# Where the last merge's raw weights lie, and when its sums begin, in a hybrid flow-matching step

## The chip, the cores and the metric

The kernel runs on one core of a Trainium2 chip. The metric is the device time in microseconds of one execution. Times inside the profiled execution count from the start of its span.

## The reference, cut to what matters

One layer with two branches (a long convolution and windowed attention) whose results are gated, projected, merged, projected once more and normalised. Only the end concerns us:

```python
def merge_branches(y_h, g_h, y_a, g_a, m, w_bh, w_ba, w_out):
    p_h = (y_h * jax.nn.silu(g_h)) @ w_bh
    p_a = (y_a * jax.nn.silu(g_a)) @ w_ba
    m_h, m_a = jnp.split(jax.nn.sigmoid(m), 2, axis=-1)
    return (m_h * p_h + m_a * p_a) @ w_out

def layer_forward(x, cond, ctx_kv, p):
...
    out = merge_branches(y_h, g_h, y_a.reshape(g_a.shape), g_a, m, p["w_bh"], p["w_ba"], p["w_out"])
    x_new = layer_norm(ALPHA * x + gate * out, p["ln_g"], p["ln_b"])
    return x_new, kv_out
```

There are 640 tokens (128 of context, 512 latent) and all widths are 1024.

## The kernel before

Activations lie transposed: channels in 128 partitions, 640 tokens along the free dimension, handled as two halves of 320. A matrix of 1024 x 1024 is eight weight tiles of 128 x 1024, numbered in one array `wall`: 80 to 87 are `w_bh` (`T_BH`), 88 to 95 are `w_ba` (`T_BA`), 96 to 103 are `w_out` (`T_WO`).

**Three matmuls for one.** For precision each fp32 operand is split into a high part, rounded to fp32r by a copy on ScalarE (ACT), and a low part, the difference from it, usually by a subtraction on VectorE (DVE). `split` (L100 to L102) does both. A product is then high·high + high·low + low·high. For some tiles the low part is made otherwise (L1163 to L1166): ACT writes the negated high part, and a transfer issued on GpSimd's queue (POOL) adds the raw weights to it from DRAM.

**Seven products for eight.** `pair_tile` (L1178) multiplies two neighbouring weight tiles `i0, i1` (four quarters a11, a12, a21, a22 of 128 x 512) with two halves of the tokens by a scheme of the Strassen-Winograd kind: seven products instead of eight, numbered j = 0 to 6 here, each of 12 matmuls of 320 columns (four K tiles, three parts each), so 84 for a pair. Four of the seven operands are sums of quarters, made on DVE by `wsum` in `prepare` (L1145) and put in tiles `s`; products 0, 4 and 5 use the quarters a11, a12, a22 as they are. `prep(j)` splits operand j into `wb[j]`. These tiles come from two rings, "wh" with two buffers (products 0, 3, 5) and "wl" with three (1, 2, 4, 6), so that product 5's place is free when product 0 of the same pair is done, and product 4's when product 6 of the pair before is done. `prep(j + 5)` for products 5 and 6 stands behind products 0 and 1; the rest stands in `prepare`. In this last merge, from the second pair on, operands 4 and 5 get their low part by the transfer on POOL.

The products are collected in four PSUM banks (`sp`, named x, y, v, z) by additions on DVE (L1204, L1210), and each finished quarter of the result goes to `use`. In the last merge that is `merged`: a gate on DVE in place of the row `ma` (L574), then `finish`, which adds the first branch's row `mh` (L1489) and splits the sum into the operands `mH, mL` of the output projection. The next pair's first product takes the bank that product 4 of this pair leaves, so it waits for that product's gate.

**The order.** TensorE's order inside the merge is that of the program. SP's loads are pinned in program order (`pinned`, L62 to L66), so a load that waits for its buffer holds back all loads behind it. The other engines' orders, and where output matmuls go among the merge's, are laid out ahead of time by a planner that simulates the program and takes, at each point, the first instruction in program order that would be ready. Each queue then runs strictly in that order. An instruction may be pinned behind what was traced before it on its engine; in `prepare` the first sum of the next pair (`wsum(2, ...)`) is.

**The stage.** First the eight tiles of `w_bh` (one `proj` each, 48 matmuls), with the rows of the attention branch loaded and split beside them, and in the end the first `w_ba` tiles loaded. `gate_bias` (L1433) adds a row to the output gates meanwhile; its raw row `b0` lies in the buffer with the tag "gr". Then four pairs of `w_ba`: (88, 89) is pair 0, (94, 95) pair 3. Raw tiles go through three buffers (tag "raw"). In the loop of `pair_tile`, each product yields twice, after its second K tile and at its end, so that the caller counts i = 0 to 13; `prepare` of the following pair stands behind product 3. The last pair starts loading and splitting the output weights (`out_weight`), whose raw tiles use the same three buffers and whose parts go where operands of the merge were. Then five output tiles of 128 tokens (`out_tile`) with a normalisation each.

Of the kernel before, what the change touches and what calls it, by code (L numbers as in the profile page):

```python
# [9 lines left out]
F32 = mybir.dt.float32  # L10
F32R = mybir.dt.float32r
# [4 lines left out]
D = 1024  # L16
# [3 lines left out]
NT = 640  # L20
# [25 lines left out]
def tile_hyena_natten_step(ctx: ExitStack, tc: tile.TileContext, a, o):  # L46
# [15 lines left out]
    def load_to(dst, src):  # L62
        ins = nc.sync.dma_start(dst, src)
        last[:] = [ins]
        if pinned[0]:
            tc.keep_in_program_order(ins)  # L66
# [33 lines left out]
    def split(dst_h, dst_l, src, eng=None):  # L100
        hi = nc.scalar.activation(dst_h, src, AF.Copy)  # L101
        return hi, (eng or nc.vector).tensor_tensor(dst_l, src, f(dst_h), op=ALU.subtract)  # L102
# [30 lines left out]
    def wraw(i):  # L133
        raws[i] = wp.tile([P, 1024], F32, tag="raw", bufs=3, name=f"raw{i}")
        load_to(raws[i][:], a["wall"][i])
# [1006 lines left out]
    def prepare(i0, i1, pin):  # L1142
        for i in (i0, i1):
            if i not in raws:
                wraw(i)  # L1145
                loads[i] = last[0]
        ra, rb = raws.pop(i0), raws.pop(i1)
        a11, a12, a21, a22 = (r[:, 512 * h : 512 * h + 512] for r in (ra, rb) for h in range(2))
        src = {0: a11, 4: a12, 5: a22}
        wb = {}  # L1150
        s_cols = 512 if i0 >= T_BH else NT

        def wsum(j, x, y, op, dst=None):
            src[j] = dst if dst is not None else sp.tile([P, s_cols], F32, tag="s", bufs=3 if i0 >= T_BH else 2, name=f"s{j}_{i0}")[:, :512]
            ins = nc.vector.tensor_tensor(src[j], x, y, op=op)  # L1155
            if pin and j == 2:
                tc.keep_in_program_order(ins)

        def prep(j):
            if j > 6:  # L1160
                return
            wb[j] = wp.tile([P, 2, 512], F32R, tag=RING[j % 5], bufs=2 if RING[j % 5] == "wh" else 3, name=f"wb{i0}_{j}")
            if i0 > T_BA and j in (4, 5):  # L1163
                nc.scalar.activation(wb[j][:, 1], src[j], AF.Copy, scale=-1.0)
                nc.gpsimd.dma_start(wb[j][:, 1], a["wall"][i0 + (j == 5)][:, 512 * (j > 0) : 512 * (j > 0) + 512], accum_op=ALU.add)
                high[i0, j] = nc.scalar.activation(wb[j][:, 0], src[j], AF.Copy)  # L1166
            else:
                high[i0, j] = split(wb[j][:, 0], wb[j][:, 1], src[j])[0]

        wsum(2, a11, a21, ALU.subtract)  # L1170
        wsum(1, src[2], a22, ALU.subtract)
        for j in range(3):
            prep(j)
        wsum(3, a21, a22, ALU.add)
        wsum(6, a12, src[1], ALU.add, src[1])
        for j in range(3, 5):
            prep(j)
        ready[i0] = wb, prep  # L1178

    def pair_tile(i0, i1, use, operand=operand):  # L1180
        def halfrow(tag, bufs, name):
            return sp.tile([P, HALF if i0 >= T_BH else 384], F32, tag=tag, bufs=bufs, name=f"{name}{i0}")[:, :HALF]

        if i0 not in ready:
            prepare(i0, i1, False)
        wb, prep = ready.pop(i0)
        ps = {}
        for j in range(7):
            if j < 4:
                ps["xyvz"[j]] = acc(f"sp{i0}_{j}")[:, :HALF]  # L1190
            dst, x = ps["xyvzxvz"[j]], operand(ORDER[j])
            for k in range(4):
                wh, wl = (wb[j][:, i, P * k : P * k + P] for i in range(2))
                for i, (wk, xi) in enumerate(((wh, 0), (wh, 1), (wl, 0))):
                    nc.tensor.matmul(  # L1195
                        dst, wk, x(xi, k), start=j < 4 and k == 0 and i == 0, stop=k == 3 and i == 2, skip_group_check=True,
                    )
                if k == 1:
                    yield
            if j == 0:  # L1200
                u = halfrow("u", 1, "u")
                nc.scalar.activation(u, dst, AF.Copy)
            elif j == 1:
                nc.vector.tensor_tensor(u, dst, u, op=ALU.add)  # L1204
            elif j == 4:
                use(0, 0, dst)
            else:
                if j != 3:
                    c = halfrow("c", 4, f"c{j}_")
                after = nc.vector.tensor_tensor(c, dst, c if j == 3 else u, op=ALU.add)  # L1210
                if j != 2:
                    use(*{3: (1, 1), 5: (1, 0), 6: (0, 1)}[j], c)
            prep(j + 5)
            if j == 3 and i0 in GATED_AT:
                gate_row(after)
                gate_load()
            if j == 3 and (i0, i1) in follow:
                prepare(*follow[i0, i1], True)
            yield

# [155 lines left out]
    nc.gpsimd.memset(eps[:], LN_EPS)  # L1376
    ts = {t: [lp.tile([P, 4, HALF], F32R, tag=f"{t}{i}", name=f"ya_{t}{i}") for i in range(2)] for t in ("t4", "t2", "t3", "t1")}

    def out_weight(k):
        raw = wp.tile([P, D], F32, tag="raw", bufs=3, name=f"wo{k}")  # L1380
        load_to(raw[:], a["wall"][T_WO + k])
        if k in (0, 1, 2, 4):
            t = {0: "t2", 1: "t3", 2: "t1", 4: "t4"}[k]
            wh, wl = (lp.tile([P, 4 * HALF], F32R, tag=f"{t}{i}", name=f"wo{k}_{i}")[:, :D] for i in range(2))
        elif k == 3:
            wh = slot(0, "v", f"woh{k}", F32R)[:, :D]
            wl = gp.tile([P, D], F32R, tag="gr", name=f"wol{k}")[:]
        else:
            if k == 5:
                wh = hp.tile([P, NK * NT], F32R, tag="hH", name="woh5")[:, :D]  # L1390
            else:
                wh = wp.tile([P, D], F32R, tag="wh", name=f"woh{k}")[:]
            if k == 5:
                wl = wp.tile([P, D], F32R, tag="raw", bufs=3, name="wol5")[:]
            else:
                wl = wp.tile([P, D], F32R, tag="wl", bufs=3, name=f"wol{k}")[:]
        wo[k] = wh, wl
        split(wh, wl, raw[:])

    def turned_sums(k):  # L1400
        b11, b12 = (ya_raw[k][:, cs] for cs in CS)
# [47 lines left out]
    with tc.manual_schedule(engines={mybir.EngineType.PE}):  # L1449
        for gen in firsts:  # L1450
            for _ in range(4):
                next(gen)
        firsts = [now(gen) for gen in firsts]
        for n in range(NK):
            ps = firsts[n] if n < 2 else now(proj(T_BH + n, yhH, yhL))
            wraw(T_BH + n + 2)
            if n % 2 == 0:
                mhp.append(mp.tile([P, 2 * NT], F32, tag=f"mh{n}", name=f"mh{n}"))
            load_to(mh(n), mh_d[n])
            for p, cs in zip(ps, CS):  # L1460
                gate(mh(n)[:, cs], p)
            if n < NK - 2:
                early[T_BH + n + 2] = wtile(T_BH + n + 2)
            ya_row(YA[n])
            if n == 0:
                gb = gate_bias()
            if n >= 2:
                next(gb, None)
        mH, mL = yhH, yhL

        mas, pending = {}, []

        def ma(n):
            if n // 2 % 2:
                mas[n] = slot(1, ("q", "ql")[n % 2], f"ma{n}")
            else:
                mas[n] = row(mp, "ma", f"ma{n}", bufs=2)
            load_to(mas[n][:], ma_d[n])

        def merged(n, hf, src):  # L1480
            th = mas[n][:, CS[hf]]
            gate(th, src)
            pending.append((n, hf, th))

        def finish():
            if not pending:
                return
            n, hf, th = pending.pop(0)
            nc.vector.tensor_tensor(th, th, mh(n)[:, CS[hf]], op=ALU.add)  # L1489
            split(mH[n][:, CS[hf]], mL[n][:, CS[hf]], th)  # L1490

        first_out = {3: 0, 5: 1, 7: 2, 9: 3}
        pairs = [(T_BA + 2 * p, T_BA + 2 * p + 1) for p in range(4)]
        for x, y in zip(pairs, pairs[1:]):
            follow[x] = y
        for p, (i0, i1) in enumerate(pairs):
            for i in (1, 0):
                ma(2 * p + i)
            for i, _ in enumerate(pair_tile(i0, i1, lambda i, hf, src: merged(2 * p + i, hf, src), ya_operand)):
                if i in (1, 3, 5, 7):  # L1500
                    finish()
                if p == 3 and i in first_out:
                    out_weight(first_out[i])
        while pending:
            finish()
        for k in (4, 6, 7, 5):
            out_weight(k)
# [193 lines left out]
```

## Time and profile before

| | us |
|---|---|
| median of 3 runs | 872.32 (872.19 to 874.64) |
| the profiled execution's own time | 874.13 |
| its span, first to last instruction | 872.1 |
| TensorE busy in the span | 857.2 |
| DVE / ACT / POOL busy in the span | 677.0 / 467.6 / 140.4 |

How to read the rows below: in a row of the timeline stand the start, the length in us, engine, line, operation, output<-inputs, the shapes, a count if rows were merged, and in brackets how long the engine idled before it and what ended that. PE is TensorE's matmul, PEld its weight load, SPq and POOLq are queues that issue transfers. A row of a list of waits says who waited for whom: us in total, times, longest. In the chain of waits stand a start, a length and what ran then. Two operations next to each other on an engine overlap a little, so a merged row is shorter than the sum of its parts.

### The profile page before, as it was taken

The page shows a single profiled execution, that of the slowest core. Times are in us where ns is not written, and L with a number is a line of the kernel's source. Part 1 is how long each engine was busy: PE and PEld are TensorE (multiplying, and loading weights), DVE is VectorE, ACT ScalarE, POOL GpSimd, SP SyncE. Part 2 cuts the span into 40 slices and gives each one's busy share as a digit, 9 for nine tenths or more (in the row PEclk, how much of TensorE's full clock was granted, in tenths as well). Part 3 has the DMA queues.
Part 4 walks back from the last instruction along what each step waited for, and adds up shares of the span by engine and source line. Part 5 has one row for each costly group of instructions (what it writes and reads, how often), then busy time and mean ns, then how long its engine had stood idle before and what let it go on. Part 6 is the DMA issues. An engine that isn't in the chain of part 4 may idle for free.

```text
span 872.1 us, 16879 instructions
## 1 busy us (share of the span) xinstructions
PE 857.2 (98%) x6394; PEld 827.7 (95%) x6394; DVE 677.0 (78%) x1404; ACT 467.6 (54%) x1004; POOL 140.4 (16%) x149
## 2 busy tenths in 40 slices
PE   8999999999999999999999999999999999999996
PEld 6899999999999999999999999999999999998885
DVE  4576678669668756899988898888879678798776
ACT  3486554645645453647665566656656554355300
POOL 0211010101001001105222225124222200010000
PEclk9999999999999999999999999999999999999999
DMA  8977756556665667764353535354263476346721
GB/s 301 387 214 173 140 124 137 127 137 152 126 143 129 132 145 177 185 222 152 104 181 100 192 93 187 106 175 154 94 182 109 136 277 209 118 120 193 253 84 50
DMA packets 59172, 139.96 MB, mean 160 GB/s; under 512 B 8751, under 2 KB 25267, under 8 KB 59092
## 3 DMA queue, kind: packets, MB, share of 16 engines
q1 hardware_dynamic: 47140, 111.69, 38.7%
q0 software_dynamic: 6336, 21.50, 15.1%
q10 hardware_dynamic: 5616, 5.70, 1.9%
q8 instruction: 50, 0.82, 0.4%
q14 instruction: 30, 0.25, 0.1%
HBM read 122.74 MB, written 16.12 MB: 159 GB/s over the span
## 4 chain that ended last, share of the span: by engine, by line
PE 93%; DMA 4%; DVE 1%; ACT 1%; issue 0%; SPq 0%; DVEq 0%; ACTq 0%
PE mm L170 32%; PE sp L1195 30%; PE out L1525 6%; PE v L926 5%; PE pt L1028 3%; PE s L1035 3%; PE s L988 2%; DMA ada<-wada 2%; PE mm L184 2%; PE ve L938 1%; DMA wo<-wall 1%; DMA wb<-wall 1%; DMA raw<-wall 1%; PE adaT L253 1%; PE yb L159 1%; PE yb L158 1%
## 5 line engine op out<-in xcount | busy, mean ns | idle before, releaser
L1195 PE MATMUL sp<-t,wb 128*128 128x320 f32 x912 | 142.0, 310 | 0.0
L1195 PEld LDWEIGHTS sp<-t,wb 128*128 128x128 f32 x912 | 135.2, 188 | 0.9 <-ACT pp L1056 0.5
L170 PE MATMUL mm<-hH,wh 128*128 128x320 f32 x480 | 113.6, 314 | 0.3 <-ACT hH L370 0.3
L170 PE MATMUL mm<-hL,wh 128*128 128x320 f32 x480 | 113.5, 312 | 0.0
L170 PE MATMUL mm<-hH,wl 128*128 128x320 f32 x480 | 113.2, 311 | 0.0
L1195 PE MATMUL sp<-hH,wb 128*128 128x320 f32 x456 | 111.2, 314 | 0.0
L170 PEld LDWEIGHTS mm<-hH,wh 128*128 128x128 f32 x480 | 80.5, 189 | 2.6 <-issue 1.4
L170 PEld LDWEIGHTS mm<-hL,wh 128*128 128x128 f32 x480 | 81.3, 189 | 0.9 <-DVE hL L378 0.4
L170 PEld LDWEIGHTS mm<-hH,wl 128*128 128x128 f32 x480 | 81.4, 189 | 0.8 <-DMA wl<-wall 0.2
L150 POOL DMA_DIRECT2D wl<-wall x38 | 33.1, 871 | 299.7 <-ACT wl L149 224.1
L1195 PEld LDWEIGHTS sp<-hH,wb 128*128 128x128 f32 x456 | 78.5, 188 | 2.3 <-issue 2.1
L151 ACT ACTIVATE wh<-raw 128x1024 fp32r<-128x1024 f32 x38 | 40.4, 1062 | 72.3 <-PE mm L170 65.2
L101 ACT ACTIVATE wb<-s 128x512 fp32r<-128x512 f32 x92 | 56.0, 628 | 39.8 <-DVE s L1155 26.6
L1195 PE MATMUL sp<-hL,wb 128*128 128x320 f32 x228 | 70.4, 309 | 0.0
L102 DVE TENSOR_TENSOR wb<-s,wb 128x512 fp32r<-128x512 f32 x92 | 62.0, 689 | 8.1 <-ACT wb L101 8.1
L101 ACT ACTIVATE wb<-raw 128x512 fp32r<-128x512 f32 x63 | 39.6, 628 | 47.6 <-PE sp L1195 24.2
L1010 POOL TENSOR_SCALAR p<-p,sm 128x384 f32<-128x384 f32 x32 | 44.7, 1409 | 101.6 <-DVE sm L1009 101.6
L102 DVE TENSOR_TENSOR wb<-raw,wb 128x512 fp32r<-128x512 f32 x63 | 44.2, 701 | 5.8 <-ACT wb L101 5.6
L170 PE MATMUL mm<-yhs,wh 128*128 128x320 f32 x256 | 47.9, 309 | 0.0
L1210 DVE TENSOR_TENSOR c<-sp,u 128x320 f32<-128x320 f32 x69 | 33.3, 482 | 12.7 <-PE sp L1195 12.7
L1195 PEld LDWEIGHTS sp<-hL,wb 128*128 128x128 f32 x228 | 42.9, 188 | 0.0
L1010 POOL TENSOR_SCALAR edge<-edge,sm 128x320 f32<-128x320 f32 x32 | 42.3, 1334 | 0.5 <-DVE sm L1009 0.5
(384 smaller groups left out, 2058.2 us busy)
## 6 DMA issues: line engine op xcount, KB each, us to landing
raw<-wall SPq DMA_DIRECT2D x93, 512.0 KB, 3.7
wl<-wall POOLq DMA_DIRECT2D x38, 512.0 KB, 5.7
ada<-wada SPq DMA_DIRECT2D x16, 512.0 KB, 7.0
tm<-bias SPq DMA_DIRECT2D x16, 512.0 KB, 4.4
gate<-wgate SPq DMA_DIRECT2D x8, 512.0 KB, 3.7
wo<-wall SPq DMA_DIRECT2D x8, 512.0 KB, 5.0
xt<-xT SPq DMA_DIRECT2D x8, 320.0 KB, 7.7
dec<-decay SPq DMA_DIRECT2D x20, 128.0 KB, 3.3
```

The source lines that it names most:

```text
L101: hi = nc.scalar.activation(dst_h, src, AF.Copy)
L102: return hi, (eng or nc.vector).tensor_tensor(dst_l, src, f(dst_h), op=ALU.subtract)
L150: nc.gpsimd.dma_start(wl, a["wall"][i], accum_op=ALU.add)
L151: nc.scalar.activation(wh, raw[:], AF.Copy)
L170: nc.tensor.matmul(ps[hf][:, :HALF], wt[k], x[:, hf * HALF : (hf + 1) * HALF], start=(i == 0 and k == 0), stop=(i == lead[2] and k == NK - ...
L926: nc.tensor.matmul(ps[t // 2][:, t % 2 * 256 : t % 2 * 256 + 256], x[:, k, P * t : P * t + P], wk, start=first and t % 2 == 0, stop=last, ...
L1010: nc.gpsimd.tensor_scalar_mul(pv, pv, sm[:, 2:3])
L1028: nc.tensor.transpose(pt[:, i * P : i * P + P], x, ident)
L1035: nc.tensor.matmul(dst, lhs, rhs, start=start, stop=stop, skip_group_check=True)
L1195: nc.tensor.matmul(dst, wk, x(xi, k), start=j < 4 and k == 0 and i == 0, stop=k == 3 and i == 2, skip_group_check=True,)
L1210: after = nc.vector.tensor_tensor(c, dst, c if j == 3 else u, op=ALU.add)
L1525: ins = nc.tensor.matmul(dst, m[k][:, c0 : c0 + P], w[:, c : c + n], start=(first and k == 0), stop=(last and k == 5), skip_group_check=True,)
```

## The change

Three things are changed in the last merge:

- Operand 5 of pairs 1 to 3 is split on DVE, like operand 5 of pair 0. Operand 4 keeps its transfer.
- `prepare` of the following pair stands behind product 1 instead of product 3 (in this merge only).
- The second raw tile of each pair gets a place of its own, loaded early: 91 and 95 where the gate rows were (tag "gr"), 93 in a large buffer that was used before (tag "v"). Of the output weights, tiles 1, 2, 3 are loaded into rows of `mh` whose sums are done, the others into the three buffers; loading (`out_load`) is separated from splitting and asked for at points i of the last pair (`first_load`). The parts of tiles 0 to 4 change homes to suit.

```diff
-            if i0 > T_BA and j in (4, 5):
+            if i0 > T_BA and j in (4,):
                 nc.scalar.activation(wb[j][:, 1], src[j], AF.Copy, scale=-1.0)
                 nc.gpsimd.dma_start(wb[j][:, 1], a["wall"][i0 + (j == 5)][:, 512 * (j > 0) : 512 * (j > 0) + 512], accum_op=ALU.add)
                 high[i0, j] = nc.scalar.activation(wb[j][:, 0], src[j], AF.Copy)
...
-            if j == 3 and (i0, i1) in follow:
+            if j == (3 if i0 < T_BH else 1) and (i0, i1) in follow:
                 prepare(*follow[i0, i1], True)
...
+    wo_raw = {}
+    OUT_RAW = {1: 0, 2: 2, 3: 4}
+
+    def out_load(k):
+        if k in OUT_RAW:
+            wo_raw[k] = mp.tile([P, 2 * NT], F32, tag=f"mh{OUT_RAW[k]}", name=f"wo{k}")[:, :D]
+        else:
+            wo_raw[k] = wp.tile([P, D], F32, tag="raw", bufs=3, name=f"wo{k}")[:]
+        load_to(wo_raw[k], a["wall"][T_WO + k])
+
     def out_weight(k):
-        raw = wp.tile([P, D], F32, tag="raw", bufs=3, name=f"wo{k}")
-        load_to(raw[:], a["wall"][T_WO + k])
-        if k in (0, 1, 2, 4):
-            t = {0: "t2", 1: "t3", 2: "t1", 4: "t4"}[k]
-            wh, wl = (lp.tile([P, 4 * HALF], F32R, tag=f"{t}{i}", name=f"wo{k}_{i}")[:, :D] for i in range(2))
-        elif k == 3:
+        if k not in wo_raw:
+            out_load(k)
+        if 0 < k < 5:
+            wh, wl = (lp.tile([P, 4 * HALF], F32R, tag=f"{('t2', 't3', 't1', 't4')[k - 1]}{i}", name=f"wo{k}_{i}")[:, :D] for i in range(2))
+        elif k == 0:
             wh = slot(0, "v", f"woh{k}", F32R)[:, :D]
             wl = gp.tile([P, D], F32R, tag="gr", name=f"wol{k}")[:]
...
-        split(wh, wl, raw[:])
+        split(wh, wl, wo_raw[k])
...
-        first_out = {3: 0, 5: 1, 7: 2, 9: 3}
+        first_load = {0: 0, 1: 1, 2: 2, 8: 3, 9: 4}
+        first_out = {2: 0, 5: 1, 7: 2, 9: 3}
...
+        def raw_early(i, tile):
+            raws[i] = tile
+            load_to(tile[:, :D], a["wall"][i])
+            loads[i] = last[0]
+
         for p, (i0, i1) in enumerate(pairs):
+            if p == 0:
+                wraw(T_BA + 2)
+                raw_early(T_BA + 3, gp.tile([P, D], F32, tag="gr", name="raw91"))
+                raw_early(T_BA + 5, slot(0, "v", "raw93"))
             for i in (1, 0):
                 ma(2 * p + i)
             for i, _ in enumerate(pair_tile(i0, i1, lambda i, hf, src: merged(2 * p + i, hf, src), ya_operand)):
                 if i in (1, 3, 5, 7):
                     finish()
+                if i == 0 and p < 2:
+                    wraw(T_BA + 2 * p + 4)
+                if i == 2 and p == 1:
+                    raw_early(T_BA + 7, gp.tile([P, D], F32, tag="gr", name="raw95"))
+                if p == 3 and i in first_load:
+                    out_load(first_load[i])
                 if p == 3 and i in first_out:
                     out_weight(first_out[i])
```

More of the change, by code (lines that the diff above doesn't have):

```diff
@@ L1390, in out_weight @@
                 wh = hp.tile([P, NK * NT], F32R, tag="hH", name="woh5")[:, :D]
+                wl = wp.tile([P, D], F32R, tag="raw", bufs=3, name="wol5")[:]
             else:
                 wh = wp.tile([P, D], F32R, tag="wh", name=f"woh{k}")[:]
-            if k == 5:
-                wl = wp.tile([P, D], F32R, tag="raw", bufs=3, name="wol5")[:]
-            else:
                 wl = wp.tile([P, D], F32R, tag="wl", bufs=3, name=f"wol{k}")[:]
         wo[k] = wh, wl
-        split(wh, wl, raw[:])
+        split(wh, wl, wo_raw[k])
     def turned_sums(k):
```

## The prediction

> **What bounds the kernel now.** I read the page's head first, then what TensorE waited for in the stretch that the change touches (from 755 us, where the last merge begins, to the end), then the chain of waits there.
>
> ```profile
> span 872.1 us, 16879 instructions
> PE 857.2 (98%) x6394; PEld 827.7 (95%) x6394; DVE 677.0 (78%) x1404; ACT 467.6 (54%) x1004; POOL 140.4 (16%) x149
> ...
> PE sp L1195 <- DMA wb<-wall: 1.4, 2, 0.9
> PE out L1525 <- ACT wo L101: 1.0, 1, 1.0
> PE sp L1195 <- DVE wb L102: 0.2, 1, 0.2
> ```
>
> TensorE is busy for 857.2 of 872.1 us, and it does the same matmuls after the change. So only its idle time can be won. In the touched stretch its list of waits holds four waits in all (three kinds, one of them twice). Their places, from TensorE's timeline:
>
> ```profile
> 777.82 1.73 PE L1195 MATMUL sp<-ya_t,wb 128*128 128x320 f32 x10 [0.86 <-DMA wb<-wall]
> 790.90 1.73 PE L1195 MATMUL sp<-ya_t,wb 128*128 128x320 f32 x10 [0.51 <-DMA wb<-wall]
> 796.63 5.26 PE L1195 MATMUL sp<-ya_t,wb 128*128 128x320 f32 x34 [0.17 <-DVE wb L102]
> 805.34 0.50 PE L1525 MATMUL out<-wo,yhs 128*128 128x512 f32 x1 [0.99 <-ACT wo L101]
> ...
> 697.37 28.16 PE mm L170 x192
> 755.53 13.30 PE sp L1195 x91
> ```
>
> The sum is 0.86 + 0.51 + 0.17 + 0.99 = **2.53 us**, the most that this change can win. The undisturbed pace is 28.16/192 = 0.1467 us a matmul, so one pair (84 matmuls, seven products of 12) takes 12.32 us and a product 1.76 us. Pair 0 therefore ends near 767.8, pair 1 near 781.1 and pair 2 near 794.2 (each later than 12.32 by its stall).
>
> Who is late? The chain and the four transfers of pairs 1 and 2 that add into `wb` (POOL rows, then each one's time to landing, in the same order):
>
> ```profile
> 771.21 6.39 DMA raw<-wall
> 784.32 6.54 DMA wb<-wall
> 797.59 6.56 DMA wo<-wall
> ...
> 769.18 0.91 POOL L1165 DMA_DIRECT2D wb<-wall  x1 [67.67 <-DVE c L1210]
> 770.70 0.87 POOL L1165 DMA_DIRECT2D wb<-wall  x1 [0.60 <-ACT u L1202]
> 782.39 0.86 POOL L1165 DMA_DIRECT2D wb<-wall  x1 [10.83 <-ACT wb L1164]
> 784.32 0.86 POOL L1165 DMA_DIRECT2D wb<-wall  x1 [1.06 <-ACT wb L1164]
> ...
> wb<-wall POOLq DMA_DIRECT2D x1, 256.0 KB, 4.3
> wb<-wall POOLq DMA_DIRECT2D x1, 256.0 KB, 7.1
> wb<-wall POOLq DMA_DIRECT2D x1, 256.0 KB, 3.9
> wb<-wall POOLq DMA_DIRECT2D x1, 256.0 KB, 6.5
> ```
>
> The first of each two is product 4's low part, the second product 5's. The first lands in 3.9 to 4.3 us. The second, sharing the engines with the first and with a raw load, takes 6.5 to 7.1: 770.70 + 7.1 = 777.8 and 784.32 + 6.5 = 790.8, just where TensorE resumes. These two stalls are product 5's transfer.
>
> **The change part by part.** *Product 5's low part by a subtraction* (pairs 1 to 3). Removed each time: one negated copy on ACT, one POOL transfer. Added: one subtraction on DVE. Its place comes free when product 0's matmuls are done, 1.76 us into the pair; the copy and subtraction after it last 0.63 and 0.68 us by the rows below, and product 5 begins 5 x 1.76 = 8.8 us in. So there are over 5 us to spare: −0.86 and −0.51, and in pair 3 the transfer that TensorE now steps around with early output matmuls. Without that spare time (the subtraction 5 us late) the stalls would be back.
>
> The price is paid on DVE, which is the risk of this change:
>
> ```profile
> 767.85:781.14 13.29, 12.43 (x85) 12.16 (x84) 12.22 (x27) 6.83 (x14) 1.78 (x2) 1.00 0.63 169
> 781.14:794.23 13.09, 12.58 (x86) 12.32 (x85) 12.29 (x26) 6.85 (x14) 1.73 (x2) 1.00 0.64 172
> ...
> 766.26 1.68 ACT L101 ACTIVATE wb<-s 128x512 fp32r<-128x512 f32 x3 [0.53 <-DVE s L1155]
> 767.96 0.68 DVE L102 TENSOR_TENSOR wb<-s,wb 128x512 fp32r<-128x512 f32 x1
> 768.96 1.28 DVE L102 TENSOR_TENSOR wb<-s,wb 128x512 fp32r<-128x512 f32 x2
> 777.62 0.69 DVE L1155 TENSOR_TENSOR s<-raw,raw 128x512 f32<-128x512 f32 x1 [0.88 <-DMA raw<-wall]
> 778.23 0.48 DVE L574 SCALAR_TENSOR_TENSOR ma<-ma,sp 128x320 f32<-128x320 f32 x1
> ```
>
> In the windows of pairs 1 and 2 the columns are span, then busy time of PE, PEld, DVE, ACT, POOL. Two subtractions of 128x512 take 1.28 where one takes 0.68, so one more costs DVE 0.60 us. DVE's 12.2 to 12.3 us of work per pair becomes about 12.85, against 12.32 that TensorE wants: it falls behind by some 0.5 us a pair, through two pairs. How late may it be? The first thing that TensorE needs back is the accumulator of product 4: its gate ran at 778.23, while product 4 of pair 1 ended near 767.85 + 5 x 1.76 = 776.7, so it started 1.6 us after its data and took 0.5. The next pair wants the bank two products (3.5 us) after that end, so 3.5 − 1.6 − 0.5 = 1.4 us are left. A lag of two times 0.5 fits, narrowly. Bounds: no stall from it (0) on one side; on the other its whole excess of 1.0 us plus the head-of-queue waits, priced under the rivals. I take 0.1, near the lower end, since 0.88 us of DVE's time in pair 1 is a wait that the next part removes.
>
> A page of the Trainium skill speaks against this part: Perfetto Trace Analysis, section Optimizing Scalar/DVE Operations, advises moving work off DVE to other engines once it is saturated, and here work is moved onto it. The windows agree that DVE is close to saturated (12.22 of 13.29 us). By that rule the time would come out above the present one; it is the second rival.
>
> *Places of their own and earlier sums.* Now each raw tile waits for one of three buffers:
>
> ```profile
> 737.65 0.90 SPq L63 DMA_DIRECT2D ma<-ma_d  x2
> 745.08 12.80 SPq L63 DMA_DIRECT2D raw<-wall  x2
> 757.97 0.86 SPq L63 DMA_DIRECT2D ma<-ma_d  x2
> 759.04 12.50 SPq L63 DMA_DIRECT2D raw<-wall  x2
> 774.68 0.80 SPq L63 DMA_DIRECT2D ma<-ma_d  x2
> 775.53 9.31 SPq L63 DMA_DIRECT2D raw<-wall  x2
> 787.76 1.13 SPq L63 DMA_DIRECT2D ma<-ma_d  x2
> 788.94 23.86 SPq L63 DMA_DIRECT2D wo<-wall  x8
> ...
> 749.93 0.68 DVE L1446 SCALAR_TENSOR_TENSOR gbc<-b,gb 128x512 f32<-128x512 f32 x1
> 763.13 0.49 DVE L574 SCALAR_TENSOR_TENSOR ma<-ma,c 128x320 f32<-128x320 f32 x1
> 799.10 0.49 DVE L1489 TENSOR_TENSOR ma<-ma,mh 128x320 f32<-128x320 f32 x1
> ```
>
> The second tile of each pair is the last issue in its row: tile 91 at 757.5, tile 93 at 771.2 (landing 777.6, where DVE's first sum of pair 2 waited 0.88 us), tile 95 at 784.5. After the change, tile 90 goes at 745.1 as now. Tile 91 waits on SP for the gate row's buffer, last read by the DVE row at 749.93, so about 750.6. Tile 93 goes right behind it. Queued behind 91's wait are tile 93 and pair 0's two `ma` rows, moved from 737.7 to about 752; they are first read at 763.13, so 11 us cover them, and with the cover gone they would cost the landing of 4 us or so. Tile 92 then waits for its old buffer (757.5), 94 follows behind the `ma` rows, and 95 waits on SP for 91's last reader in pair 1 (near 771) with pair 2's `ma` rows behind it. 95 is wanted by the sums only after product 1 of pair 2, near 783: 12 us against a landing of 6.4.
>
> The sums of the next pair thus start behind product 1 rather than product 3, that is 3.5 us sooner, on data that has long landed. The first sum is pinned behind DVE's earlier work, and all of DVE stands behind it; that pin cost 0.88 us at 777.62 and should cost nothing now. The weights of product 1 that were late by 0.17 at 796.63 have 3.5 us more: −0.17. What stays bound is product 4's transfer: its place comes free only at the pair's start, the POOL row follows 1.3 us later (769.18 against 767.85), and TensorE wants it at its third matmul, 7.04 + 0.29 = 7.3 us in. That leaves 6.0 us for a landing of 3.9 to 4.3. The DVE end of it does not change.
>
> The Trainium skill, DMA: Bandwidth & Descriptors, section Anatomy of one DMA — SWDGE (gpsimd) path, fits such a transfer by about 2.0 us plus its bytes over 436 GB/s; as an estimate that is 2.6 us for 256 KB, and by it no stall at product 5 would exist today. The rows with 6.5 and 7.1 decide against it where transfers share the engines.
>
> *Output weights.* Now the first raw tile goes at 788.94, the second only at 797.59 (landing 6.56 us later) and the output waits 0.99 us for its split. After, the second and third go into rows of the first halves' sums (`mh0`, `mh2`), whose last readers are in pairs 1 and 2, so all three are issued within about 1 us of 788.9, some 8 us earlier for the second: −0.99. Their splits (128x1024, so about 2 x 0.6 us of DVE each) run where DVE has no next pair to prepare. The fourth waits on SP for pair 2's last addition (799.1, so free near 799.5), and tiles 4, 6, 7, 5 stand behind it. With the landing of 6.56 it is there by 806. The output may start at 755.53 + 4 x 12.32 = 804.8, and takes a weight tile in six matmuls of 512 columns, by estimate 512/320 of 0.1467 each, 1.4 us a tile: the fourth is wanted at 809.0. That is 3 us of cover for the split's copy and subtraction, about 2.4.
>
> **Sum.** −0.86 − 0.51 − 0.17 − 0.99 = −2.53, plus 0.1 for DVE and 0.1 for new small waits of an order planned afresh: −2.3. The profiled execution took 874.13 us for its span of 872.1; its own time would become 871.8. The median of the runs shown, 872.32, is 1.8 lower than the profiled one; I take the same −2.3 from it: **870.0 us**.
>
> **The rivals.** *Product 4's transfer becomes the late one.* If it meets the earlier loads it takes 6.5 to 7.1 instead of 4: 0.5 to 1.1 us of stall in each of three pairs, 1.5 to 3.3, against 2.53 won. For it: tile 95 is issued close to pair 1's start, the output tiles close to pair 3's. Against: product 4's transfers landed in 4.3 and 3.9 us with raw loads already close by. Middle 2.4: 872.2.
>
> *DVE sets the pace* (the other side). From the point where its lag passes the 1.4 us left before product 4's bank is wanted, each pair takes DVE's time. That is 12.85 plus what DVE idled in these windows, 13.29 − 12.22 = 1.07 and 13.09 − 12.29 = 0.80, together 27.6 where TensorE's two pairs now take 26.38: +1.2; the output's 0.99 stays, as its splits queue behind: 873.5. For it: 12.85 against 12.32. Against: part of that idling is the 0.88 us wait on the raw load, and 1.4 us of slack outlast two excesses of 0.5.
>
> *The change does half of what it says*: the output matmuls are put by the planner among pair 3's, as now (805.34), and meet another wait of about 1 us, or the stall of 0.99 stays: −2.3 + 1.0, 871.0.
>
> **How the numbers follow.** The forecast has 0.68, half the gain 0.14, the late transfer 0.08, DVE's pace 0.10. What a measurement of this kernel can tell from no change is about 0.3%, here 2.6 us. The largest gain, 2.53, falls just short of it, so most of the forecast lies within: faster by more than that needs nearly the whole 2.53 and a lucky tenth, 0.17, and slower beyond 874.9 only the worst of the last two cases, 0.07; within, 0.76. The forecast's own range is 869.5 to 870.8; taking in the half gain, the late transfer and most of DVE's pace: 869.4 to 873.2.
>
> **What would show it.** Right: no wait of TensorE on `wb` transfers at products 4 and 5; POOL with three transfers instead of six, near 4 us each; DVE's first sums without a DMA wait, just behind product 1; the second and third output tiles issued near 789; TensorE's idle time between 755 and the output under 0.5 us. Wrong: waits of `sp` on DVE near the start of pairs 2 and 3 (DVE's pace), waits on the transfer at product 4, or output matmuls early in pair 3 with a wait on a split.

## The result and the profile after

The changed kernel takes 869.08 us (median of 20 runs, 867.53 to 874.10), the kernel before 873.83 us (20 runs, 872.06 to 877.85): ratio 0.9943, interval 0.9929 to 0.9957. That is 0.57% faster, about 5 us, where 2.3 were forecast. The three runs shown before the prediction (872.32) lay at the low end of what the kernel before does. The first profiled execution of the changed kernel took 871.15 us with a span of 869.3.

```profile
span 869.3 us, 16872 instructions
PE 856.0 (98%) x6394; PEld 827.1 (95%) x6394; DVE 678.7 (78%) x1407; ACT 465.5 (54%) x1001; POOL 137.8 (16%) x146
```

Three transfers of POOL and three ACT copies are gone, three operations of DVE have come. Next the chain of waits from the merge's first product to the first DVE work after the last output matmul, first of the kernel before, then of the changed one:

```profile
755.53 13.30 PE sp L1195 x91
...
810.07 54.14 PE out L1525 x257
...
864.24 0.43 DVE r L1540
```

```profile
756.26 45.83 PE sp L1195 x312
802.09 2.10 PE out L1548 x9
804.19 1.76 PE sp L1195 x12
805.95 2.10 PE out L1548 x9
808.04 1.76 PE sp L1195 x12
809.80 51.60 PE out L1548 x246
...
861.43 0.43 DVE r L1563
```

After the change the chain is TensorE without a gap. I call this stretch the tail. It takes 864.24 − 755.53 = 108.71 us before and 861.43 − 756.26 = 105.17 after: 3.54 us less, although the matmuls are the same and the four waits read before the prediction sum to 2.53. (The merge began 0.73 us later in this execution. The shift arises in the first 71 us of the kernel and stays the same from there on; it differs between executions of both kernels.)

**Where the missing microsecond is.** The next view shows the same four waits of the kernel before as TensorE's weight loads have them:

```profile
777.81 1.47 PEld L1195 LDWEIGHTS sp<-ya_t,wb 128*128 128x128 f32 x10 [1.13 <-DMA wb<-wall]
790.90 1.47 PEld L1195 LDWEIGHTS sp<-ya_t,wb 128*128 128x128 f32 x10 [0.77 <-DMA wb<-wall]
796.62 5.00 PEld L1195 LDWEIGHTS sp<-ya_t,wb 128*128 128x128 f32 x34 [0.44 <-DVE wb L102]
805.34 0.19 PEld L1525 LDWEIGHTS out<-wo,yhs 128*128 128x128 f32 x1 [1.43 <-ACT wo L101]
```

They sum to 3.77. A matmul's row is about 0.31 us long while the next begins after 0.147, so the idle time ahead of a matmul counts only from the end of a row that overlaps the wait by 0.16 to 0.19 us: with that, 2.53 becomes 3.21. And behind each of the four waits the next matmul follows 0.10 to 0.13 us later than at the usual pace, 0.45 in all. Start to start the loss is therefore 3.66, near the 3.54 of the tails. The windows of both tails (span, then busy time of PE, PEld, DVE, ACT, POOL) show the part that hides in busy rows: 1.00 us, for the same matmuls.

```profile
755.53:864.24 108.71, 106.13 (x601) 95.22 (x599) 86.19 (x156) 36.32 (x64) 5.24 (x6) 1.00 0.47 149
756.26:861.43 105.17, 105.13 (x601) 95.30 (x599) 87.53 (x159) 34.68 (x61) 2.64 (x3) 1.00 0.42 142
```

**DVE, pair by pair.** The windows of the four pairs after the change (span, then busy time of PE, PEld, DVE, ACT, POOL):

```profile
756.26:768.58 12.32, 12.32 (x87) 12.32 (x86) 11.21 (x22) 5.33 (x10) 0.00 (x0) 1.00 0.50 184
768.58:780.90 12.32, 12.32 (x87) 12.32 (x86) 12.05 (x26) 6.37 (x12) 0.91 (x1) 1.00 0.46 118
780.90:793.22 12.32, 12.32 (x86) 12.32 (x85) 12.23 (x27) 6.72 (x13) 0.87 (x1) 1.00 0.37 81
793.22:809.80 16.58, 16.58 (x104) 15.71 (x103) 16.14 (x30) 11.71 (x18) 0.86 (x1) 1.00 0.69 235
```

Every pair takes 12.32 us. DVE is busy for 98 to 99% of the second and third and carries the rest into the last. Product 4's gate and the next pair's first sum, from DVE's timeline:

```profile
774.02 0.68 DVE L1155 TENSOR_TENSOR s<-raw,raw 128x512 f32<-128x512 f32 x1
777.63 0.48 DVE L574 SCALAR_TENSOR_TENSOR ma<-ma,sp 128x320 f32<-128x320 f32 x1
786.24 0.69 DVE L1155 TENSOR_TENSOR s<-raw,raw 128x512 f32<-128x512 f32 x1
790.65 0.48 DVE L574 SCALAR_TENSOR_TENSOR ma<-ma,sp 128x320 f32<-128x320 f32 x1
```

Product 4 ends 8.80 us into a pair, at 777.38 and 789.70: the gate ran 0.25 and then 0.95 us later. The lag grows by 0.7 us from the one pair to the next and stays below the 1.6 us that it was in the kernel before.

### The profile page after: what moved, and what is told of

Read it like the earlier page. It is cut to its first block, busy times and chain, and to the rows that moved or that the text cites. A ratio compares the mean times of both kernels' runs of the same rounds, so it can differ in the third digit from the quotient of the medians.

```text
span 869.3 us, 16872 instructions
## 1 busy us (share of the span) xinstructions
PE 856.0 (98%) x6394; PEld 827.1 (95%) x6394; DVE 678.7 (78%) x1407; ACT 465.5 (54%) x1001; POOL 137.8 (16%) x146
## 4 chain that ended last, share of the span: by engine, by line
PE 96%; DMA 3%; DVE 1%; ACT 0%; POOL 0%; issue 0%; DVEq 0%; POOLq 0%
PE sp L1195 33%; PE mm L170 31%; PE out L1548 6%; PE v L926 5%; PE pt L1028 3%; PE s L1035 3%; PE s L988 2%; PE mm L184 2%; DMA ada<-wada 2%; PE ve L938 1%; DMA wl<-wall 1%; PE adaT L253 1%; PE adaT L270 1%; PE yb L159 1%; PE yb L158 1%; PE yb L160 1%
## 5 line engine op out<-in xcount | busy, mean ns | idle before, releaser
L101 ACT ACTIVATE wb<-raw 128x512 fp32r<-128x512 f32 x66 | 41.5, 628 | 47.3 <-PE sp L1195 23.4
L102 DVE TENSOR_TENSOR wb<-raw,wb 128x512 fp32r<-128x512 f32 x66 | 46.5, 704 | 5.1 <-ACT wb L101 4.8
```

## The experiments

Ratios are to the kernel before on the same chip, with 95% intervals. Two theories at first: A, the gain is the stalls of the tail and nothing else; B, these stalls differ from run to run and the first profile caught short ones.

**1. Both kernels again.** No edit.

> The kernel before, once more. Theory A (the gain is TensorE's stalls in the last merge and nothing else, 3.5 us of the profiled execution): ratio 1.000, and in this second profile the same four stalls, summing to 3.3 to 3.8 us by the weight loads' rows. Rival B (the stalls of product 5's transfers vary from run to run and the first profile caught short ones): ratio 1.000, but another size of those two stalls, together more than 3 us. Rival C (the rest of the gain is luck of the start, where the weights of the modulation land): the merge begins more than 1 us later or earlier than at 755.5.

> The changed kernel, once more. Theory A: ratio to before 0.9960 (3.5 of 873). Rivals B and C: 0.994 to 0.995 again under B, anything from 0.993 to 0.998 under C. In the second profile all three expect no wait of TensorE between 740 us and the end.

Measured: 0.9999 (0.9984 to 1.0015) and 0.9948 (0.9927 to 0.9968). The second profile of the kernel before, weight loads again:

```profile
775.54 1.48 PEld L1195 LDWEIGHTS sp<-ya_t,wb 128*128 128x128 f32 x10 [1.17 <-DMA wb<-wall]
788.69 1.47 PEld L1195 LDWEIGHTS sp<-ya_t,wb 128*128 128x128 f32 x10 [0.81 <-DMA wb<-wall]
794.42 5.00 PEld L1195 LDWEIGHTS sp<-ya_t,wb 128*128 128x128 f32 x34 [0.44 <-DVE wb L102]
804.23 0.19 PEld L1525 LDWEIGHTS out<-wo,yhs 128*128 128x128 f32 x1 [2.53 <-ACT wo L101]
```

The same four places, but 4.95 us: the wait for the second output weight is 1.1 us longer. The changed kernel's second profile has one wait, which no theory expected: 0.45 us on product 4's transfer in pair 3.

**2. Two more profiles of the kernel before.** No edit, one execution each.

> The kernel before, a third profile. The stretch from the merge's first product to the last output tile's last matmul took 108.7 and 109.9 us in two profiles. If the first was a short one, this one is nearer to 109.9, with the wait for the second output weight above 1.43 us; if the second was a long one, nearer to 108.7.

> The kernel before, a fourth profile: the same question as for the third.

The first of these executions took 2002 us, with matmul rows of about 570 ns where 310 is usual; why is not known, and it says nothing on the question. The other:

```profile
775.85 1.47 PEld L1195 LDWEIGHTS sp<-ya_t,wb 128*128 128x128 f32 x10 [1.93 <-DMA wb<-wall]
789.18 1.47 PEld L1195 LDWEIGHTS sp<-ya_t,wb 128*128 128x128 f32 x10 [1.02 <-DMA wb<-wall]
794.90 4.99 PEld L1195 LDWEIGHTS sp<-ya_t,wb 128*128 128x128 f32 x34 [0.44 <-DVE wb L102]
804.05 0.19 PEld L1525 LDWEIGHTS out<-wo,yhs 128*128 128x128 f32 x1 [1.87 <-ACT wo L101]
```

That is 5.26 us. The waits on transfers and on the output weight vary, the wait on DVE does not. The tail by the chains of all profiles:

| kernel | merge begins | last output done | tail |
|---|---|---|---|
| before, three profiles | 755.53, 753.22, 752.76 | 864.24, 863.13, 862.93 | 108.7, 109.9, 110.2 |
| changed, two profiles | 756.26, 752.53 | 861.43, 858.10 | 105.2, 105.6 |

The means, 109.6 and 105.4, are 4.2 us apart. So the gain is A's stalls, and the first profile of the kernel before was the shortest of three, as B has it in kind. B's own sign was not met: product 5's two stalls sum to 1.90, 1.98 and 2.95 us, never above 3, and the output weight's wait varies as much. C's sign was met, since the merge of the kernel before began 2.3 and 2.7 us before 755.53 in the later profiles, but in the changed kernel it moves as much. 4.2 of 873 is a ratio of 0.9952, inside the interval.

**3. Product 5 alone, and product 5 undone.**

```diff
 # the kernel before
-            if i0 > T_BA and j in (4, 5):
+            if i0 > T_BA and j in (4,):
```

```diff
 # the changed kernel
-            if i0 > T_BA and j in (4,):
+            if i0 > T_BA and j in (4, 5):
```

> The kernel before with only product 5's low part made on DVE; loads and sums as before. Theory A: the two stalls on transfers go (1.13 + 0.77 by the weight loads' rows), the waits at 796.6 and 805.3 (0.44 + 1.43) stay or the first grows by the sums' late loads: ratio 0.9978 (1.9 us). Rival B: 0.996 or less. A third theory, D (DVE cannot take it while its sums still wait for the raw loads): ratio 0.999 to 1.002, new waits of sp on DVE.

> The changed kernel with product 5's low part made by the transfer again; early loads and sums stay. Theory A: the stalls on transfers come back in pairs 1 and 2, and in pair 3 where nothing is put in their way: two or three of 0.7 to 1.1 us, so 1.9 to 2.8 us above the changed kernel, ratio to before 0.998 to 0.999. Rival B: 3 us or more above the changed kernel.

Measured: 0.9979 (0.9963 to 0.9996) and 0.9978 (0.9961 to 0.9995). The first is as A has it in time and cause. The second is near A in its ratio, but its median lies 3.4 us above the changed kernel's on the same chip (872.05 against 868.68), which is B's figure, and its waits are in part others than A's. With product 5 alone on DVE the two stalls on transfers are gone and the late sums show more (0.88 instead of 0.44):

```profile
782.24 4.99 PEld L1195 LDWEIGHTS sp<-ya_t,wb 128*128 128x128 f32 x34 [0.88 <-DVE wb L102]
802.78 0.19 PEld L1525 LDWEIGHTS out<-wo,yhs 128*128 128x128 f32 x1 [0.94 <-ACT wo L101]
```

With it undone, one stall on product 5 came back, in pair 1 and not in pair 2. POOL's rows for product 5 in these pairs, then the first one's landing in the chain and the waits:

```profile
768.60 0.87 POOL L1165 DMA_DIRECT2D wb<-wall  x1 [0.84 <-DVE ma L1496]
782.07 0.86 POOL L1165 DMA_DIRECT2D wb<-wall  x1 [0.90 <-DVE yhs L102]
...
768.60 7.09 DMA wb<-wall
...
775.73 1.47 PEld L1195 LDWEIGHTS sp<-ya_t,wb 128*128 128x128 f32 x10 [1.14 <-DMA wb<-wall]
799.26 0.30 PEld L1195 LDWEIGHTS sp<-ya_hH,wb 128*128 128x128 f32 x2 [0.64 <-DMA wb<-wall]
806.67 0.19 PEld L1548 LDWEIGHTS out<-wo,yhs 128*128 128x128 f32 x1 [2.08 <-ACT wo L101]
```

In pair 1, tile 95 was loaded at 768.78, 0.18 us after the transfer's issue, and the transfer took 7.09 us. In pair 2 nothing was loaded beside the transfer; it took 5.7 us and landed in time. Product 4's transfer was under way in both. So what makes product 5 late is a raw load that leaves just behind its transfer, on top of product 4's.

The other two waits are not on product 5. The 0.64 us are on product 4's transfer in pair 3, the 2.08 on the fourth output weight, whose load left only at 799.36: its place is a row of `mh`, and the last addition that reads this row ended just before.

**4. One part taken back at a time.**

```diff
 # late_sums: the changed kernel
-            if j == (3 if i0 < T_BH else 1) and (i0, i1) in follow:
+            if j == 3 and (i0, i1) in follow:
```

```diff
 # out_ring: the changed kernel
-    OUT_RAW = {1: 0, 2: 2, 3: 4}
+    OUT_RAW = {}
...
-        first_load = {0: 0, 1: 1, 2: 2, 8: 3, 9: 4}
+        first_load = {}
```

```diff
 # no_transfer: the changed kernel
-            if i0 > T_BA and j in (4,):
+            if False:
```

> The changed kernel with the next pair's sums behind product 3 again; loads in their own places, product 5 on DVE. Theory A: the raw tiles have landed, so no wait on a load; but DVE, busy for over 12 of every 12.32 us, comes to the sums 3.5 us later, and product 1's weights are late in one or two pairs by 0.4 to 0.9 us: ratio to before 0.9955 to 0.9965 (changed kernel 0.9945). Rival E (starting sooner is worth nothing once the loads are early): 0.994 to 0.995, no wait of sp on DVE.

> The changed kernel with all raw output weights in the three shared buffers, each loaded only when its split is traced. Theory A: the wait for the second output weight (1.43 and 2.53 us by the weight loads' rows in two profiles of the kernel before) is cured by the places of their own: it comes back in part, 0.5 to 1.5 us, ratio 0.9955 to 0.9965. Rival F (it was cured by the buffers that the raw tiles of the pairs no longer hold): 0.994 to 0.995 and no wait of out.

> The changed kernel with product 4's low part on DVE as well, so no transfer adds into wb at all. DVE's work per pair grows by 0.60 to about 13.4 us against TensorE's 12.32. Theory D (DVE sets the pace once its lag has used up the 1.4 us of slack): two or three pairs 1 us longer, 1.5 to 3 us above the changed kernel, ratio to before 0.9965 to 0.998, waits of sp on DVE. Rival H (the slack in the order takes it up): 0.994 to 0.995.

Measured: 0.9980 (0.9964 to 0.9996), 0.9965 (0.9946 to 0.9985) and 0.9956 (0.9940 to 0.9973). Late sums cost more than A gave them: most of the gain is lost. By the weight loads' rows TensorE waited 0.88 and 0.43 us for product 1's low part, as A has it, but also 1.58 us in pair 3 for product 1's copy on ACT, which stood behind the split of the first output weight, and 1.09 us for the low part of that weight. The buffers for the output weights cost about what A has, but not as it has it: the output did not wait, TensorE waited 1.88 us for product 4's transfer in pair 3 (landing in 7.82 us among the output loads), and the interval includes no loss at all. Without transfers TensorE waited little, though DVE had 0.60 us more per pair:

```profile
789.99 0.19 PEld L1195 LDWEIGHTS sp<-ya_hH,wb 128*128 128x128 f32 x1 [0.30 <-ACT wb L101]
802.43 1.76 PEld L1195 LDWEIGHTS sp<-ya_t,wb 128*128 128x128 f32 x12 [0.39 <-DVE c L1210]
```

So the trace does not show D's 1.5 to 3 us; whether this kernel is slower than the changed one at all, its interval leaves open.

**5. The sums alone.**

```diff
 # the kernel before
-            if j == 3 and (i0, i1) in follow:
+            if j == (3 if i0 < T_BH else 1) and (i0, i1) in follow:
```

> The kernel before with only the point of the sums moved, behind product 1; loads in the three shared buffers, product 5 by transfer. Theory A: the data come no sooner than their buffer, so the sums cannot start before the landing: ratio 0.999 to 1.001, the first sum waiting longer at the head of DVE's queue. Rival G (the first sum is pinned and blocks DVE until the load lands): new waits of 1 us and more on DVE's work, ratio 1.002 to 1.006.

Measured: 0.9946 (0.9927 to 0.9966), 869.19 us. Both expectations fell: this one line, with the old buffers and with product 5's transfers, brings the whole gain, as far as the intervals tell. (It moves all of `prepare`, the splits behind the sums too; no run separates them.) Its tail is 859.53 − 754.20 = 105.3 us, with 0.40 us of waits left:

```profile
801.09 1.47 PEld L1195 LDWEIGHTS sp<-ya_t,wb 128*128 128x128 f32 x10 [0.16 <-DMA wb<-wall]
803.33 0.30 PEld L1525 LDWEIGHTS out<-wo,yhs 128*128 128x128 f32 x2 [0.24 <-DVE wo L102]
```

How? A raw tile's load waits until the tile that had its buffer before has been read for the last time. The kernel before (DVE, ACT, DVE, SP, then what SP's queue waited for last before this load), and below it the kernel with the sums alone (DVE, ACT, SP, POOL):

```profile
766.15 0.68 DVE L1155 TENSOR_TENSOR s<-raw 128x512 f32<-128x512 f32 x1
...
770.56 0.63 ACT L1166 ACTIVATE wb<-raw 128x512 fp32r<-128x512 f32 x1
...
770.96 0.68 DVE L1155 TENSOR_TENSOR s<-raw,s 128x512 f32<-128x512 f32 x1
...
771.21 0.33 SPq L63 DMA_DIRECT2D raw<-wall  x1
...
SPq L63 <- ACT wb L1166: 4.3, 1, 4.3
```

```profile
764.05 0.69 DVE L1155 TENSOR_TENSOR s<-raw,s 128x512 f32<-128x512 f32 x1
...
767.16 0.61 ACT L1166 ACTIVATE wb<-raw 128x512 fp32r<-128x512 f32 x1
...
757.70 10.42 SPq L63 DMA_DIRECT2D raw<-wall  x2
...
769.36 0.87 POOL L1165 DMA_DIRECT2D wb<-wall  x1 [0.84 <-DVE yhs L102]
```

Before, tile 93's load waited for the sum at 766.15 and then for ACT's copy of operand 5, which ended at 770.56 + 0.63 = 771.19. Both read tile 91, so 93 went into 91's buffer. Tile 90's buffer came free later still: the last sum of the pair (`s<-raw,s`) reads tile 90 and ended at 771.6. Product 5's transfer is issued between ACT's two copies of operand 5 (at 770.70), so a load that waits for the second copy leaves right behind it, here by 0.5 us, and the transfer took 7.1 us. With sooner sums tile 90's buffer is held only until ACT's copy of operand 4 at 767.8; tile 93 leaves then (757.70 + 10.42 − 0.33), 1.6 us ahead of the transfer, which lands in 5.1. In both kernels the load has the buffer that came free first. In the same way the second output weight waited for ACT's copy of operand 5 in pair 3 before (797.57) and for that of operand 4 now: its load left 792.45 − 754.20 = 38.3 us into the merge instead of 797.59 − 755.53 = 42.1. So the late sums were the root of all four waits: they made product 1's weights late and kept the first tile's buffer, which put the raw load behind the transfer and held back the output weight. That their place cures all four is shown by this run; the way from sum to load is read from these rows. It fits `p5_undone` too: there tile 95's place is tile 91's, whose last reader is ACT's copy of operand 5 again (it ended at 768.76), so that its load left right behind the transfer in spite of sooner sums.

**6. What the other parts add.** Theory J is this root; K, that the parts add up. `p5_sums` is the kernel before with the edits of 5 and of product 5 (3, first diff); `places_alone` the changed kernel with `late_sums` and with product 5's transfer (3, second diff).

> The kernel before with the sums behind product 1 and product 5 on DVE, raw tiles in the three shared buffers. Theory J (the late sums were the root: they kept a raw buffer, so the next raw load left late, met product 5's transfer, and the output weights' load was held too; sooner sums alone cure all four waits): nothing is left to win over the sums alone, ratio 0.994 to 0.996, no wait above 0.5 us. Rival K (each of the three parts adds its own gain): 0.991 to 0.993.

> The changed kernel with the sums behind product 3 and product 5 by transfer, so only the places and the loads' order are new. Theory J: tile 95 is loaded when 91's last reader in pair 1 is done, right on product 5's transfer, so pair 1's stall of about 1.1 us stays, pair 2's goes (its transfer has no raw load beside it), product 1's late weights stay: ratio 0.997 to 1.000. Rival K: 0.9965 or less, as the loads alone would bring the output weight's 1.4 to 2.5 us.

Measured: 0.9946 (0.9930 to 0.9963) and 1.0020 (1.0003 to 1.0037). K is refuted by the first, which has no wait left and is no faster than the sums alone. J expected the places alone at 0.997 to 1.000, and they are slower than that, by two waits that J did not have. ACT's rows in pair 3, and TensorE's weight loads:

```profile
793.36 1.06 ACT L101 ACTIVATE woh<-wo 128x1024 fp32r<-128x1024 f32 x1 [2.66 <-DMA wo<-wall]
794.32 1.14 ACT L101 ACTIVATE wb<-s 128x512 fp32r<-128x512 f32 x2
...
794.98 0.30 PEld L1195 LDWEIGHTS sp<-ya_t,wb 128*128 128x128 f32 x2 [2.12 <-ACT wb L101]
...
807.55 0.19 PEld L1548 LDWEIGHTS out<-wo,yhs 128*128 128x128 f32 x1 [3.17 <-ACT wo L101]
```

The split of the first output weight stands in ACT's queue ahead of product 1's copy and waits 2.66 us for its load, with TensorE behind it. The larger wait, 3.17 us, is the output's for its fourth weight: as in `p5_undone`, the load into the row of `mh` left only behind the addition that reads that row, at 799.83. The eight combinations of the three parts:

| | no part | product 5 on DVE | places | both |
|---|---|---|---|---|
| sums behind product 3 | 1 | 0.9979 | 1.0020 | 0.9980 |
| sums behind product 1 | 0.9946 | 0.9946 | 0.9978 | 0.9943, 0.9948 |

Read downwards: the sums bring 0.3 to 0.5% in every column. Read across: the places bring nothing and cost 0.2 to 0.3% where product 5 keeps its transfer; product 5 on DVE brings 0.2 to 0.4% except where the sums alone have already cured its wait. No kernel here beats the changed one by more than the intervals allow.

## Why the prediction was right and wrong

- *Only TensorE's idle time can be won*: right as far as the runs tell. The gain is the tail's waits (4.2 us by the tails, of 4.75 by the medians), and they are gone.
- *"2.53 us, the most that this change can win"*: this term failed, and with it the forecast of 870.0, the range (869.4 was its low end) and the 0.17 given to a gain above 0.3%. The waits were right in place and in what ended them, but mis-sized. Read from the rows of the matmuls they were 2.53; by the tails of the two first profiles 3.54, because 1.0 us of the stalls hides in busy rows; over three profiles of the kernel before against two of the changed one 4.2, because the waits on transfers and loads were shorter in the first profile than in the others. That 870.0 still lies within 1 us of the measured 869.08 is luck: it was counted from 872.32, and the same −2.3 from the later median of 873.83 gives 871.5.
- *The parts*: −1.37 for product 5, −0.17 for the sums, −0.99 for the places. This split failed. Each wait was costed to the part that names its last releaser. The runs give the whole gain to the sums alone, 0.9979 to product 5 alone and a loss to the places alone. The step "that pin cost 0.88 us at 777.62" saw that the sums were late, but not what they did to the loads: the sum at 770.96 still held tile 90's buffer, so the load of 771.21 had to wait for ACT's copy of operand 5 and left right behind product 5's transfer.
- *Product 5 late because "sharing the engines with the first and with a raw load"*: right, shown by `p5_undone` (7.09 us with the load 0.18 us behind, 5.7 and in time without). The Trainium skill, DMA: Bandwidth & Descriptors, section Issuing engines are not separate DMA queues, has transfers of all issuers run on the same 16 engines and interleave; the 7.1 us of this transfer among others, where 3.9 to 4.6 were enough ahead of them, agree.
- *Product 4's transfer as the late one*: a small part of it is real, 0.45 us in one of two profiles of the changed kernel, in pair 3 among the output loads as that rival had it; in `out_ring` it was 1.88.
- *DVE sets the pace*: did not happen. DVE is as full as worked out and its lag grew by 0.7 us from pair to pair (0.5 forecast), but it began at 0.25 us, not at the 1.6 from which the slack of 1.4 was counted. The Trainium skill, Perfetto Trace Analysis, section Optimizing Scalar/DVE Operations, says that it may make sense to move some work off a saturated DVE; here even a further 0.60 us per pair (`no_transfer`) left waits of only 0.30 and 0.39 us.
- *Loads and order*: tiles 91, 93, 92 and 95 were issued as worked out (751.4, 751.8, 758.3 and 772.2, in an execution whose merge began 0.73 us later). The first three output loads were not: they left at 791.1, 791.6 and 793.3 instead of near 789, behind an `ma` row's load of 790.76. They were early enough, and no output matmul met a wait.

## What to carry to other kernels

Where several waits stand in a row, follow the buffer of each late load back to its last reader, and ask why no other buffer was free sooner, before costing the waits one by one: here one late sum held a buffer, and the load that had to take the next one disturbed a transfer. Size a stall of TensorE from start to start against the undisturbed pace (or from the weight loads), and from more than one profile when a transfer ends it. An engine that is 99% busy need not set the pace as long as what TensorE needs next stands early in its queue.

## What the runs showed of the hardware

The same 256 KB transfer, adding into on-chip memory, took 3.9 to 4.6 us in the kernel before when it was the first of its pair. Issued 1.8 and 1.9 us behind such a transfer, with no load leaving beside it, it took 5.7 and 5.3 (pair 2 of `p5_undone` and `places_alone`); with a 512 KB load leaving 0.2 to 0.5 us behind it as well, 6.5 to 8.0 (the kernel before, nine transfers in three profiles). With the load issued 1.6 us before it instead it took 5.1 and 5.3 (the sums alone, pairs 1 and 2): which goes first changes it by 1 to 3 us. Load landings at the same place differed between executions of one program by over a microsecond (the second output weight's load: 6.56, 7.66 and 7.00 us), and the merge began between 752.8 and 755.5 us in three executions of the kernel before.
